# The inverse root mean square of eighteen norms, by one wide matmul and a power instead of column sums, Newton steps and a spread

## The chip, the cores and the metric

The kernel runs on one core of a Trainium2 chip. A core has a matmul engine (TensorE, in the profile PE, with its weight loads as PEld), VectorE (DVE), ScalarE (ACT), GpSimd (POOL) and SyncE (SP), which issues most of the DMAs. Each engine takes its instructions in order, and they wait for one another by semaphores. The metric is the device time of one execution in microseconds.

## The reference

One decoder layer in float32 with 2048 tokens (SEQ) and 1024 channels (D_MODEL). What matters here is that it has five RMS norms.

```python
def rmsnorm(x, g):
    xf = x.astype(jnp.float32)
    r = lax.rsqrt(jnp.mean(xf * xf, axis=-1, keepdims=True) + EPS)
    return (xf * r * g.astype(jnp.float32)).astype(x.dtype)

hn = rmsnorm(h, norm1_g)
proj = jnp.einsum('bsd,de->bse', hn, w_in)      # 512 pool channels, q, k, v
y_pool = pool_mixer(u_pool, pool_w, pool_scale)
o = stick_breaking_attention(to_heads(q), to_heads(k), to_heads(v))
mixed = jnp.concatenate([rmsnorm(y_pool, pool_out_g), rmsnorm(y_attn, attn_out_g)], axis=-1)
h = h + jnp.einsum('bse,ed->bsd', mixed, w_out)
hn2 = rmsnorm(h, norm2_g)
up = jnp.einsum('bsd,df->bsf', hn2, w_up)       # 4096 channels
act = jnp.square(jax.nn.relu(up))
h = h + jnp.einsum('bsf,fd->bsd', act, w_down)
return rmsnorm(h, final_g)
```

## The kernel before

The tokens are cut into four tiles of T = 512, and channels lie on the 128 partitions, so a tile of activations is a row of chunks of 128x512, one per 128 channels. Large products are made of float32r matmuls in three parts: `split` cuts an operand into a high and a low half (ScalarE rounds, line 143; VectorE subtracts, line 144), and a product is high x high, high x low and low x high.

The program runs in stages. The front (to about 500 us of the span) makes the input projection, the pool mixer and the attention of the four tiles, interleaved; the tail (to about 700 us) makes the output projection and the second norm; then `up` (to about 1290 us) and `down` (to the end) are the two halves of the feed-forward part, each a fast matrix multiplication of seven block products.

In front and tail the order is written by hand. `step` puts a dense product (`dense`, two granules of weights, 24 matmuls of 128x512 into one of two PSUM banks "pd") on a list; `run` goes through the list, and after each product `catch_up` takes a few pieces of elementwise work from the queue `later` (squares, norms, scaling of chunks), and `advance` a share of the attention. Weights are split five granules ahead (`WAHEAD`). A scheduler with a timeline of assumed costs then orders the instructions of each engine; `issue_after` and `gates` pin some of them: a gate makes the products that come a certain number of granules later wait for a norm's matmuls in the order of TensorE.

A norm goes so. The squares of the chunks are added up elementwise into `ss` (128x512), so that what is left is a sum over partitions, that is a column sum. `mean_squares` takes it with four float32 matmuls, each with 128 columns of `ss` as stationary side and a column of 1/n as moving side (line 199): the result `pm` is 128x4, tokens on partitions. `inv_root` adds the epsilon on VectorE (line 207) and takes the inverse root by a guess from the bits (line 208) and three Newton steps (lines 211 to 218), on the engine it is given. The result is cut into two float32r parts `yr` (lines 235 and 236), and `spread` (line 225) brings it back to all partitions with eight matmuls against the identity, in which the four columns are broadcast as stationary side; `pr` is 128x512, and ScalarE copies it to `r` in SBUF (line 245). VectorE then scales the chunks by gain and `r` (lines 257, 823, 917 and 1151).

There are 21 such roots: thirteen by `inv_rms` on GpSimd (front and tail), one by `inv_rms` on VectorE (the very first, in `norm1_first`), two by `root_last` for the two last tiles (their parts lie in `yrlast` until `up` spreads them, lines 1021 to 1024), three by `final_root` and `final_put` in `down`, and two halves of the last tile in `finish`, on VectorE, without a spread.

GpSimd has otherwise small copies (lines 371, 376 and 654) and, in `down`, the residual adds of `add_residual` (line 1096).

Of the kernel before, what the change touches and what calls it, by code (L numbers as in the profile page):

```python
# [8 lines left out]
F32 = mybir.dt.float32  # L9
F32R = mybir.dt.float32r  # L10
BF16 = mybir.dt.bfloat16
I32 = mybir.dt.int32
AF = mybir.ActivationFunctionType
ALU = mybir.AluOpType

P = 128
S = 2048
D = 1024
T = 512
# [8 lines left out]
TB = T // P  # L28
# [4 lines left out]
EPS = 1e-6  # L33
# [13 lines left out]
def hymba_block(ctx: ExitStack, tc: tile.TileContext, xT, gains, w_in, pool_w, w_out, w_up, w_down, out):  # L47
    nc = tc.nc
# [3 lines left out]
    const = pool("const", 1)  # L52
# [38 lines left out]
    open_big(left_scope)  # L91


    zero = ntp.tile([P, T], F32, tag="nt", name="zero")
    nc.vector.memset(zero, 0.0)
    ident = const.tile([P, P], F32, name="ident")
# [23 lines left out]
    zeros = const.tile([1, 1], I32, name="zeros")  # L120
    rlast = const.tile([P, 2, T], F32, name="rlast")
    sslast = const.tile([P, T], F32, name="sslast")
    yrlast = const.tile([P, 2, 2, TB], F32R, name="yrlast")
    carry = const.tile([P, len(WINDOWS), PAD], F32, name="carry")
    nc.vector.memset(carry, 0.0)

# [20 lines left out]
    marks, gates = {}, []  # L147
# [46 lines left out]
    def mean_squares(parts, n, where=None, tag="px"):  # L194

        pm = (where or psx).tile([P, T], F32, tag=tag, name="pm")
        for c in range(TB):
            for i, ss in enumerate(parts):
                marks["pm"] = nc.tensor.matmul(pm[:, c:c + 1], ss[:, c * P:(c + 1) * P], inv[n],  # L199
                                               start=(i == 0), stop=(i == len(parts) - 1))  # L200
        return pm[:, 0:TB]

    def inv_root(pm, eng):

        v, w = vp.tile([P, 3 * TB], F32, tag="v", name="v"), pm.shape[-1]
        m, y, t = v[:, 0:w], v[:, TB:TB + w], v[:, 2 * TB:2 * TB + w]
        nc.vector.tensor_scalar(m, pm, 1.0, EPS, op0=ALU.mult, op1=ALU.add)
        eng.tensor_scalar(y.bitcast(I32), m.bitcast(I32), -0.5, float(0x5F3759DF), op0=ALU.mult, op1=ALU.add)
        for _ in range(3):
            if eng is nc.vector:  # L210
                eng.scalar_tensor_tensor(t, y, -0.5, y, op0=ALU.mult, op1=ALU.mult)
                eng.tensor_tensor(t, t, m, ALU.mult)
                eng.scalar_tensor_tensor(y, t, 1.5, y, op0=ALU.add, op1=ALU.mult)
            else:
                eng.tensor_tensor(t, y, y, ALU.mult)
                eng.tensor_tensor(t, t, m, ALU.mult)
                eng.tensor_scalar(t, t, -0.5, 1.5, op0=ALU.mult, op1=ALU.add)
                eng.tensor_tensor(y, y, t, ALU.mult)
        return y

    def spread(pr, yr):

        for b in range(TB):
            for x in range(2):
                mm = nc.tensor.matmul(pr[:, b * P:(b + 1) * P], yr[:, x, b:b + 1].to_broadcast([P, P]), identr,  # L225
                                      start=(b == 0 and x == 0), stop=(b == TB - 1 and x == 1), skip_group_check=True)
        return mm

    def inv_rms(ss, n, r=None, eng=None, early=False):

        eng = eng or nc.gpsimd
        with tc.high_priority():
            y = inv_root(mean_squares([ss], n, psz if early else None, "pz" if early else "px"), eng)
            yr = tmp.tile([P, 2, TB], F32R, tag="yr", name="yr")
            eng.tensor_copy(yr[:, 0], y)
            eng.tensor_tensor(yr[:, 1], y, yr[:, 0].bitcast(F32), ALU.subtract)
            where, tag = (psx, "px") if eng is nc.vector else (psz, "pz") if early else (pst, "pt")
            pr = where.tile([P, T], F32, tag=tag, name="pr")
            marks["pr"] = spread(pr, yr)
            if eng is not nc.vector:  # L240
                g = state["tick"]
                gates.extend([(g + 10, marks["pm"]), (g + 14, marks["pr"])])
            if r is None:
                r = tmp.tile([P, T], F32, tag="r", name="r", bufs=2)
            nc.scalar.activation(r, pr, AF.Copy)
            return r

# [43 lines left out]
    todo, begun, finished, state = [], {}, set(), {"gran": 0, "tick": 0, "due": 0.0}  # L291
# [519 lines left out]
        return took  # L811

    def root_last(i, ss, where=None, tag="px"):
        y = inv_root(mean_squares([ss], D, where, tag), nc.gpsimd)
        nc.gpsimd.tensor_copy(yrlast[:, i, 0], y)
        nc.gpsimd.tensor_tensor(yrlast[:, i, 1], y, yrlast[:, i, 0].bitcast(F32), ALU.subtract)

    def norm2(j):
        acc = [st[j]["acc"][:, k] for k in range(KD)]
# [35 lines left out]
    def up(pools, more):  # L855
# [18 lines left out]
        def load(q, m):  # L874
            raw[q, m] = (rbb if m % 2 else rba).tile([P, 4, G, P], F32, tag="rb", name="rb")
            nc.sync.dma_start(raw[q, m], w_up[m])
# [9 lines left out]
        def make_weights(g):  # L886
            q, m, s = slots[g]
            which, i = what[s][1]
            if s == "P2":
                add_weights(q, m)  # L890
            hl = hlp.tile([P, 2, G, P], F32R, tag="hw", name="hw", align_bytes=256)
            split((hl[:, 0], hl[:, 1]), (sums if which else raw)[q, m][:, i])
            ops[g] = hl

        def make_left(q, s):
            i, parts = what[s][0], []
            for c in range(2):
                r = srp.tile([P, 2, T], F32, tag="sr", name="sr")
                nc.sync.dma_start(r, su[q][i][c])
                t = saps[order.index(s)].tile([P, 2, 2, T], F32R, tag="sa", name="sa", align_bytes=256)  # L900
                split((t[:, 0], t[:, 1]), r)
                parts.append(t)
            left_ops[q, s] = parts
# [97 lines left out]
        rbb, pup, avp, psu = more()  # L1001
        load(0, 1)
        lefts = [(g, q, s) for g, (q, m, s) in enumerate(slots) if m == 0 and not (q == 0 and s in order[:LB])]
        for g, (q, m, s) in enumerate(slots):
            while lefts and lefts[0][0] <= g + LA:
                make_left(*lefts.pop(0)[1:])
            if q == 0 and 4 <= m < 12 and m % 2 == 0 and s in SUMS:
                sums_second(m // 2 - 2, SUMS.index(s))
            bank, first, last = what[s][2:]
            if first:  # L1010
                ps[q, m, bank] = psu.tile([P, T], F32, tag=bank, name="p" + bank)
            t, w = ps[q, m, bank], ops.pop(g)
            for c in range(G):
                a = left_ops[q, s][c // 2]
                for x, (wx, ax) in enumerate(((0, 0), (0, 1), (1, 0))):
                    nc.tensor.matmul(t, w[:, wx, c], a[:, ax, c % 2], start=first and c == 0 and x == 0,  # L1016
                                     stop=last and c == G - 1 and x == 2, skip_group_check=True)
            post(q, m, s)
            if g == 1:
                root_last(1, sslast, psu, "R")  # L1020
            elif g in (6, 10):
                pr, i = psu.tile([P, T], F32, tag="R", name="pr"), g // 10
                spread(pr, yrlast[:, i])
                nc.scalar.activation(rlast[:, i], pr, AF.Copy)
            if g + UA < len(slots):
                make_weights(g + UA)
                q2, m2, s2 = slots[g + UA]
                n = q2 * NM + m2 + 2
                if s2 == "P3" and n < 2 * NM:
                    load(*cols[n])  # L1030

    def down(pools):
        t8, s8, rs, rt, pup, rsp, rlp, tmp_, psb = pools
# [103 lines left out]

        def final_root(j, acc, ss, r):

            y = inv_root(mean_squares([ss], D, psb, f"b{free}"), nc.gpsimd)  # L1140
            yr = tmp_.tile([P, 2, TB], F32R, tag="yr", name="yr", bufs=3)
            nc.gpsimd.tensor_copy(yr[:, 0], y)
            nc.gpsimd.tensor_tensor(yr[:, 1], y, yr[:, 0].bitcast(F32), ALU.subtract)
            roots.append((j, acc, r, yr))

        def final_put(j, acc, r, yr):
            pr = psb.tile([P, T], F32, tag=f"b{free + 1}", name="pr")
            spread(pr, yr)
            nc.scalar.activation(r, pr, AF.Copy)
            for k in range(KD):  # L1150
                nc.vector.scalar_tensor_tensor(acc[k], acc[k], gf[:, k:k + 1], r, op0=ALU.mult, op1=ALU.mult)
                nc.sync.dma_start(out[j, k], acc[k])

        finals, roots, lastv = [], [], {}
# [80 lines left out]
        free, held = 4, []  # L1235
        for g in range(DA):
            make(g)
        for g, (n_, i, kk, qs_) in enumerate(steps):
            if g + DA < len(steps):
                make(g + DA)  # L1240
            t, left_ = made.pop(g)
# [3 lines left out]
            for q in qs_:  # L1245
                for n in range(4):
                    if kk == 0 and n_ in ("P1", "P5", "P2"):
                        ps[q, n] = bank(4 * q + n)
                    for c in range(2):
                        for x, (wx, ax) in enumerate(((0, 0), (0, 1), (1, 0))):  # L1250
                            nc.tensor.matmul(ps[q, n], t[:, wx, c, n * P:(n + 1) * P], left_[q][:, ax, c],  # L1251
                                             start=(n_ in ("P1", "P5", "P2") and kk == 0 and c == 0 and x == 0),
                                             stop=(n_ in ("P4", "P3", "P2") and kk == 7 and c == 1 and x == 2),
# [3 lines left out]
            if n_ == "P2":  # L1257
                if qs_ == (1,):
                    free = 0
# [169 lines left out]
```

## Time and profile before

| | |
|---|---|
| median of 3 runs | 1945.07 us (1943.7 to 1950.17) |
| span of the profiled execution | 1941.4 us; the page gives no separate time for it |
| PE busy | 1922.7 us, 99% |
| DVE busy | 1267.6 us, 65% |
| ACT busy | 956.9 us, 49% |
| POOL busy | 192.0 us, 10% |
| DMA | 426.79 MB, mean 220 GB/s |
| granted TensorE clock | 0.998 of full speed |

The profile is of one execution. A row of a tile or a line has the count, the durations in ns and the first and last start in us; a row of the chain has the start, the length and the work that carried the end in that time; a row of the timeline has start, length, engine, line, operation, output and inputs, and in brackets the idle time of the engine before it.

### The profile page before, as it was taken

The numbers are of one execution on the slowest core, as the hardware profiler recorded it, in microseconds if no ns is written. First come the engines' busy times: TensorE is split into PE (matmuls) and PEld (weight loads), VectorE is DVE, ScalarE is ACT, GpSimd is POOL, SyncE is SP. The second block draws the span as 40 slices with busy tenths as digits, with TensorE's granted clock in tenths as the row PEclk, the third lists the DMA queues.
The fourth block names the chain that finished last, engine by engine and source line by source line (L and its number), as shares of the span: only waits on it lengthen the run. The fifth ranks groups of instructions, "written<-read, shape, count | busy, mean of one in ns | idle before, by whom it ended". The sixth has DMA issues, their size and how long they took to land.

```text
span 1941.4 us, 25998 instructions
## 1 busy us (share of the span) xinstructions
PE 1922.7 (99%) x9139; PEld 1605.2 (83%) x9139; DVE 1267.6 (65%) x1882; ACT 956.9 (49%) x1544; POOL 192.0 (10%) x399
## 2 busy tenths in 40 slices
PE   9999999999999999999999999999999999999997
PEld 7888888888888888888888888878888888888887
DVE  6887799668876975777586565665454443446474
ACT  5565566455544555555575555553323233424353
POOL 0211123102111110000000000000110000213010
PEclk9999999999999999999999999999999999999999
DMA  6685686888696954677564544477885554546472
GB/s 216 206 273 180 223 279 208 266 307 285 235 378 233 338 187 155 213 243 247 181 243 159 173 141 158 145 268 288 290 284 196 192 196 151 201 153 208 148 255 89
DMA packets 164845, 426.79 MB, mean 220 GB/s; under 512 B 19680, under 2 KB 25824, under 8 KB 160608
## 3 DMA queue, kind: packets, MB, share of 16 engines
q1 hardware_dynamic: 164560, 424.77, 64.1%
q8 instruction: 74, 1.21, 0.3%
q14 instruction: 67, 0.55, 0.1%
q10 hardware_dynamic: 144, 0.26, 0.0%
HBM read 284.44 MB, written 140.51 MB: 219 GB/s over the span
## 4 chain that ended last, share of the span: by engine, by line
PE 94%; DVE 3%; DMA 2%; ACT 1%; issue 0%; SPq 0%; DVEq 0%; ACTq 0%
PE pb L1251 31%; PE pY L1016 17%; PE pd L173 8%; PE pd L172 8%; PE pd L174 8%; PE pZ L1016 8%; PE pX L1016 4%; PE po L669 2%; PE pta L658 1%; PE pm L199 1%; PE pz L611 1%; PE pz L612 1%; PE pr L225 1%; DMA wr<-in_w_down_dram 1%; PE pb L1214 1%; PE pz L640 0%
## 5 line engine op out<-in xcount | busy, mean ns | idle before, releaser
L1251 PE MATMUL pb<-ad,wd 128*128 128x512 f32 x2640 | 601.6, 390 | 1.3 <-ACT ad L143 0.7
L1251 PEld LDWEIGHTS pb<-ad,wd 128*128 128x128 f32 x2640 | 494.8, 188 | 104.6 <-ACT ad L143 1.3
L1016 PE MATMUL pY<-sa,hw 128*128 128x512 f32 x1536 | 364.3, 390 | 1.2 <-ACT u L955 1.2
L1016 PEld LDWEIGHTS pY<-sa,hw 128*128 128x128 f32 x1536 | 288.1, 188 | 61.8 <-ACT u L955 2.1
L172 PE MATMUL pd<-h,hl 128*128 128x512 f32 x752 | 299.8, 399 | 0.7 <-DVE qkr L418 0.7
L173 PE MATMUL pd<-h,hl 128*128 128x512 f32 x752 | 297.2, 395 | 0.0
L174 PE MATMUL pd<-h,hl 128*128 128x512 f32 x752 | 297.0, 395 | 0.0
L143 ACT ACTIVATE ad<-ar 128x1024 fp32r<-128x1024 f32 x112 | 117.4, 1051 | 139.4 <-PE pb L1251 116.7
L1016 PE MATMUL pZ<-sa,hw 128*128 128x512 f32 x768 | 184.6, 389 | 0.0
L144 DVE TENSOR_TENSOR ad<-ar,ad 128x1024 fp32r<-128x1024 f32 x112 | 144.3, 1293 | 55.6 <-ACT ad L143 55.6
L144 DVE TENSOR_TENSOR wd<-wr,wd 128x1024 fp32r<-128x1024 f32 x64 | 82.2, 1285 | 148.9 <-ACT wd L143 148.4
L143 ACT ACTIVATE wd<-wr 128x1024 fp32r<-128x1024 f32 x64 | 67.8, 1059 | 206.0 <-PE pb L1251 198.3
L1016 PEld LDWEIGHTS pZ<-sa,hw 128*128 128x128 f32 x768 | 144.1, 188 | 29.8
L172 PEld LDWEIGHTS pd<-h,hl 128*128 128x128 f32 x752 | 142.2, 189 | 28.3 <-DVE qkr L418 1.0
L174 PEld LDWEIGHTS pd<-h,hl 128*128 128x128 f32 x752 | 141.9, 189 | 27.9
L173 PEld LDWEIGHTS pd<-h,hl 128*128 128x128 f32 x752 | 142.0, 189 | 26.8
L143 ACT ACTIVATE hl<-raw 128x512 fp32r<-128x512 f32 x168 | 104.2, 630 | 108.2 <-PE pd L174 69.9
L144 DVE TENSOR_TENSOR hl<-raw,hl 128x512 fp32r<-128x512 f32 x168 | 114.6, 687 | 51.3 <-ACT hl L143 50.9
L144 DVE TENSOR_TENSOR hw<-rt,hw 128x512 fp32r<-128x512 f32 x128 | 87.7, 688 | 76.3 <-ACT hw L143 76.1
L1016 PE MATMUL pX<-sa,hw 128*128 128x512 f32 x384 | 93.1, 389 | 0.0
L1046 DVE TENSOR_TENSOR wr<-wr 128x1024 f32<-128x1024 f32 x32 | 39.2, 1224 | 81.0 <-DMA wr<-in_w_down_dram 78.0
L955 ACT ACTIVATE u<-pY 128x512 f32<-128x512 f32 x64 | 38.1, 595 | 103.6 <-PE pY L1016 103.3
(203 smaller groups left out, 2389.7 us busy)
## 6 DMA issues: line engine op xcount, KB each, us to landing
ar<-sd SPq DMA_DIRECT2D x112, 512.0 KB, 4.5
wr<-in_w_down_dram SPq DMA_DIRECT2D x72, 512.0 KB, 3.7
rb<-in_w_up_dram SPq DMA_DIRECT2D x32, 1024.0 KB, 6.1
sd<-a SPq DMA_DIRECT2D x128, 256.0 KB, 3.7
raw<-in_w_in_dram SPq DMA_DIRECT2D x50, 512.0 KB, 4.4
sd<-s SPq DMA_DIRECT2D x96, 256.0 KB, 3.8
raw<-in_w_out_dram SPq DMA_DIRECT2D x32, 512.0 KB, 5.6
sr<-su SPq DMA_DIRECT2D x28, 512.0 KB, 5.5
```

The costliest lines, as they stand in the source:

```text
L143: nc.scalar.activation(hi, src, AF.Copy)
L144: return nc.vector.tensor_tensor(lo, src, hi.bitcast(F32), ALU.subtract)
L172: nc.tensor.matmul(ps, hl[:, 0, c], hi, start=(k == 0), stop=False)
L173: nc.tensor.matmul(ps, hl[:, 0, c], lo, start=False, stop=False)
L174: mm = nc.tensor.matmul(ps, hl[:, 1, c], hi, start=False, stop=(k == n - 1))
L199: marks["pm"] = nc.tensor.matmul(pm[:, c:c + 1], ss[:, c * P:(c + 1) * P], inv[n], start=(i == 0), stop=(i == len(parts) - 1))
L225: mm = nc.tensor.matmul(pr[:, b * P:(b + 1) * P], yr[:, x, b:b + 1].to_broadcast([P, P]), identr, start=(b == 0 and x == 0), stop=(b == TB ...
L669: nc.tensor.matmul(po[:, p * 256 + to:p * 256 + to + hi - lo], vw[:, 2 * p + v], at[:, x, lo:hi], start=(p == 0 and n == 0 and x == 0), sk ...
L955: nc.scalar.activation(k[name], y, AF.Copy)
L1016: nc.tensor.matmul(t, w[:, wx, c], a[:, ax, c % 2], start=first and c == 0 and x == 0, stop=last and c == G - 1 and x == 2, skip_group_che ...
L1046: nc.vector.tensor_tensor(b, a, b, ALU.subtract)
L1251: nc.tensor.matmul(ps[q, n], t[:, wx, c, n * P:(n + 1) * P], left_[q][:, ax, c], start=(n_ in ("P1", "P5", "P2") and kk == 0 and c == 0 an ...
```

## The change

For the eighteen roots that ran on GpSimd, `mean_root` replaces `mean_squares`, `inv_root`, the parts `yr` and `spread`. A constant 128x128 matrix with 1/n everywhere is the stationary side of one float32 matmul with `ss` as moving side, so that every partition of `pm` (128x512) has the mean square of each token. ScalarE copies it to `r` and adds the epsilon, and GpSimd raises `r` to the power of -0.5 in place, with a constant column broadcast as exponent. The bank for `pr` and its gate fall away, and the roots of the last two tiles are complete at once in `rlast`. The first norm and the halves of the last tile stay as they were.

```diff
+    mean = {}
+    for n in (D, D // 2):
+        mean[n] = const.tile([P, P], F32, name=f"mean{n}")
+        nc.gpsimd.memset(mean[n], 1.0 / n)
+    root = const.tile([P, 1], F32, name="root")
+    nc.gpsimd.memset(root, -0.5)
...
-    yrlast = const.tile([P, 2, 2, TB], F32R, name="yrlast")
...
+    def mean_root(ss, n, r, where, tag):
+
+        pm = where.tile([P, T], F32, tag=tag, name="pm")
+        marks["pm"] = nc.tensor.matmul(pm, mean[n], ss, start=True, stop=True)
+        nc.scalar.activation(r, pm, AF.Copy, bias=EPS)
+        nc.gpsimd.tensor_tensor(r, r, root.to_broadcast([P, T]), ALU.pow)
+
     def inv_rms(ss, n, r=None, eng=None, early=False):
 
-        eng = eng or nc.gpsimd
         with tc.high_priority():
+            if eng is None:
+                if r is None:
+                    r = tmp.tile([P, T], F32, tag="r", name="r", bufs=2)
+                mean_root(ss, n, r, psz if early else psx, "pz" if early else "px")
+                gates.append((state["tick"] + 10, marks["pm"]))
+                return r
             y = inv_root(mean_squares([ss], n, psz if early else None, "pz" if early else "px"), eng)
...
-            where, tag = (psx, "px") if eng is nc.vector else (psz, "pz") if early else (pst, "pt")
-            pr = where.tile([P, T], F32, tag=tag, name="pr")
-            marks["pr"] = spread(pr, yr)
-            if eng is not nc.vector:
-                g = state["tick"]
-                gates.extend([(g + 10, marks["pm"]), (g + 14, marks["pr"])])
...
     def root_last(i, ss, where=None, tag="px"):
-        y = inv_root(mean_squares([ss], D, where, tag), nc.gpsimd)
-        nc.gpsimd.tensor_copy(yrlast[:, i, 0], y)
-        nc.gpsimd.tensor_tensor(yrlast[:, i, 1], y, yrlast[:, i, 0].bitcast(F32), ALU.subtract)
+        mean_root(ss, D, rlast[:, i], where or psx, tag)
...
             if g == 1:
                 root_last(1, sslast, psu, "R")
-            elif g in (6, 10):
-                pr, i = psu.tile([P, T], F32, tag="R", name="pr"), g // 10
-                spread(pr, yrlast[:, i])
-                nc.scalar.activation(rlast[:, i], pr, AF.Copy)
...
         def final_root(j, acc, ss, r):
 
-            y = inv_root(mean_squares([ss], D, psb, f"b{free}"), nc.gpsimd)
...
+            mean_root(ss, D, r, psb, f"b{free}")
+            roots.append((j, acc, r))
+
+        def final_put(j, acc, r):
...
```

More of the change, by code (lines that the diff above doesn't have):

```diff
@@ L209, in inv_root @@
         for _ in range(3):
[L210 to L218, printed above, removed]
+            eng.scalar_tensor_tensor(t, y, -0.5, y, op0=ALU.mult, op1=ALU.mult)
+            eng.tensor_tensor(t, t, m, ALU.mult)
+            eng.scalar_tensor_tensor(y, t, 1.5, y, op0=ALU.add, op1=ALU.mult)
         return y
@@ L236, in inv_rms @@
             eng.tensor_tensor(yr[:, 1], y, yr[:, 0].bitcast(F32), ALU.subtract)
-            where, tag = (psx, "px") if eng is nc.vector else (psz, "pz") if early else (pst, "pt")
-            pr = where.tile([P, T], F32, tag=tag, name="pr")
-            marks["pr"] = spread(pr, yr)
-            if eng is not nc.vector:
-                g = state["tick"]
-                gates.extend([(g + 10, marks["pm"]), (g + 14, marks["pr"])])
-            if r is None:
-                r = tmp.tile([P, T], F32, tag="r", name="r", bufs=2)
+            pr = psx.tile([P, T], F32, tag="px", name="pr")
+            spread(pr, yr)
             nc.scalar.activation(r, pr, AF.Copy)
@@ L1138, in final_root @@
         def final_root(j, acc, ss, r):
-            y = inv_root(mean_squares([ss], D, psb, f"b{free}"), nc.gpsimd)
[L1141 to L1149, printed above, removed]
+            mean_root(ss, D, r, psb, f"b{free}")
+            roots.append((j, acc, r))
+        def final_put(j, acc, r):
             for k in range(KD):
```

## The prediction

> **What bounds the kernel now.** I read the page's busy table and its chain first, to see which engine sets the end.
>
> ```profile
> span 1941.4 us, 25998 instructions
> PE 1922.7 (99%) x9139; PEld 1605.2 (83%) x9139; DVE 1267.6 (65%) x1882; ACT 956.9 (49%) x1544; POOL 192.0 (10%) x399
> PE 94%; DVE 3%; DMA 2%; ACT 1%; issue 0%; SPq 0%; DVEq 0%; ACTq 0%
> ```
>
> TensorE (PE) is busy for 99% of the span and carries 94% of the chain that ended last. A microsecond taken out of TensorE's stream is a microsecond off the end, as long as nobody else becomes late. So the first question is what the norms cost on TensorE, and the second is who could become late. For the second I cut the span by stage and keep the stretch that holds most of the norms, 30 to 660 us. The columns after the length are busy time of PE, weight loads, DVE, ACT and POOL, then granted clock, DMA share and GB/s.
>
> ```profile
> 30.00:660.00 630.00, 626.35 (x3342) 532.62 (x3343) 504.18 (x852) 346.18 (x625) 110.58 (x281) 1.00 0.77 256
> ```
>
> There VectorE (DVE) is busy 504.18 of 630 us, 80%: it has 126 us of idle time in this stretch, and it is the only engine near PE.
>
> **How many norms the change touches.** The rows of the tiles pm and v count them. In the rows of a tile the three numbers are minimum, median and maximum in ns.
>
> ```profile
> L199 PE MATMUL pm<-inv,ss x144: 165/250/251, 29.5 to 1895.9; 128*128 128x1 f32 x144
> L199 PE MATMUL pm<-inv,sslast x8: 164/250/251, 702.2 to 702.9; 128*128 128x1 f32 x8
> L207 DVE TENSOR_SCALAR v<-pm x19: 136/157/164, 31.0 to 1896.2; 128x4 f32<-128x4 f32 x19
> L208 POOL TENSOR_SCALAR v<-v x18: 192/193/2301, 63.3 to 1896.5; 128x4 int32<-128x4 int32 x18
> L218 POOL TENSOR_TENSOR v<-v x54: 198/199/1507, 64.4 to 1901.6; 128x4 f32<-128x4 f32 x54
> ```
>
> Nineteen norms read pm with VectorE; eighteen of them run their Newton steps on GpSimd (POOL): thirteen through inv_rms, two through root_last, three through final_root. Those eighteen change. The first norm and the two halves of the last tile keep Newton on VectorE. A second thing stands here: 19 norms times 4 column sums are 76 matmuls in the code, and 152 in the trace. A float32 matmul is two TensorE instructions, where the float32r ones are one.
>
> **What is removed on TensorE.** The chain gives what these groups displace, which is less than the durations, because matmuls overlap. Columns: start, length, what.
>
> ```profile
> 177.43 0.79 PE pm L199 x8
> 694.66 2.72 PE pY L1016 x12
> 1895.32 0.79 PE pm L199 x8
> 1904.38 0.06 PE pr L225
> 1904.72 0.73 PE pr L225 x7
> ```
>
> Eight column-sum instructions take 0.79 us, and eight spread matmuls take 0.06 + 0.73 = 0.79 us. Both sit on the chain, in the middle of the work. Each of the eighteen norms so gives back 1.58 us, 28.4 us together.
>
> **What is added on TensorE.** One float32 matmul of 512 columns per norm. No float32 matmul of that width is in the trace, so I bound it. A float32r matmul of 512 columns takes 2.72 / 12 = 0.227 us of the stream. Two instructions at that rate are 0.45 us: the lower end. The upper end is my estimate from the doubled count: if float32 is worked as two parts, and the two instructions are the two parts of the stationary side, the moving side may have to pass twice as well, four passes of 0.227 us, 0.91 us. The one-column matmuls cannot show it, their columns being too few. I take the upper end, since the doubled instructions show that the array does split this type. The sum is 18 x (1.58 - 0.91) = 12.1 us saved; by the lower end, 18 x (1.58 - 0.45) = 20.3 us.
>
> The Trainium skill says in "FP8 and Floating Point Precision", section TensorE Precision Notes, that true float32 takes four passes through the array; by it the sum is the same 12.1 us, and no row here shows more than the two instructions.
>
> **The other engines' small change.** Durations for this part, from the rows of r, and the timeline of GpSimd and ScalarE after the last of these norms (first and last of its fifteen GpSimd instructions):
>
> ```profile
> L245 ACT ACTIVATE r<-pr x12: 583/598/601, 39.1 to 625.1; 128x512 f32<-128x512 f32 x12
> 1896.47 0.19 POOL L208 TENSOR_SCALAR v<-v 128x4 int32<-128x4 int32 x1 [34.02 <-DVE v L207]
> 1902.12 0.20 POOL L1143 TENSOR_TENSOR yr<-v,yr 128x4 fp32r<-128x4 f32 x1
> 1905.49 0.60 ACT L1149 ACTIVATE rf<-pr 128x512 f32<-128x512 f32 x1 [1.82 <-PE pr L225]
> ```
>
> ScalarE (ACT) copied pr to r in 0.6 us; now it copies pm to r with the epsilon in 0.6 us: nothing. VectorE loses 18 x 0.157 = 2.8 us of L207, hidden under PE. GpSimd loses fifteen small instructions per norm, 5.9 us from first to last here. TensorE loses a wait on GpSimd in its in-order queue; it cost nothing, since the spread was queued late enough. Before, r was ready 10.8 us after the column sums began (1895.32 to 1906.09). The two memsets of the mean matrices run on GpSimd at the very start, where nothing but later transposes needs what follows them: nothing.
>
> **The power.** One GpSimd instruction, 128x512, two inputs, per norm. No power is in the trace. The nearest row is the residual add, of the same engine, shape and number of inputs:
>
> ```profile
> L1096 POOL TENSOR_TENSOR u<-u,res x16: 1279/1322/2209, 1673.4 to 1773.3; 128x512 f32<-128x512 f32 x16
> L1096 POOL TENSOR_TENSOR c<-c,res x8: 1288/1296/2293, 1650.4 to 1668.8; 128x512 f32<-128x512 f32 x8
> ```
>
> It cannot be shorter than the add's 1.28 us, which reads and writes the same amounts. For the upper end I take as many passes of the add as the Newton chain has arithmetic steps (one guess, three rounds of four, the epsilon): 14 x 1.28 = 18 us; a power needs a logarithm and an exponential, which are series of about such a length. These ends are far apart. I take 5 us, their geometric mean, because neither end has a row of this operation.
>
> With 5 us the new latency is 0.9 + 0.6 + 5 = 6.5 us, less than 10.8, so no consumer of r is later than before. What else it can hurt is VectorE. These rows show the residual adds beside VectorE's splits, whose normal time is the median in the first:
>
> ```profile
> L144 DVE TENSOR_TENSOR ad<-ar,ad x112: 1207/1219/2312, 1310.8 to 1899.4; 128x1024 fp32r<-128x1024 f32 x112
> 1661.39 2.22 DVE L144 TENSOR_TENSOR wd<-wr,wd 128x1024 fp32r<-128x1024 f32 x1 [0.74 <-ACT wd L143]
> 1663.53 4.55 DVE L144 TENSOR_TENSOR ad<-ar,ad 128x1024 fp32r<-128x1024 f32 x2
> 1661.22 3.54 POOL L1096 TENSOR_TENSOR c<-c,res 128x512 f32<-128x512 f32 x2 [1.97 <-DMA res<-hs]
> 1665.20 1.79 POOL L1096 TENSOR_TENSOR c<-c,res 128x512 f32<-128x512 f32 x1 [0.44 <-DMA res<-hs]
> ```
>
> While GpSimd adds, a split that takes 1.22 us takes 2.2 to 2.3, and the add in turn 1.8 instead of 1.3. Each waits out the other. So I price the power as time in which VectorE's two-input work stands still. Behind it in VectorE's in-order queue wait the evacuations of TensorE's result banks and the splits of the weights. The front has two banks for its dense products, and one bank's product is 24 matmuls, 24 x 0.227 = 5.4 us: a standstill below that is covered. Five us is covered, just. In total thirteen such standstills are 65 us, half of the 126 us that VectorE has idle there.
>
> The Trainium skill speaks against the change here: "SBUF — State Buffer", section Who interferes with whom, says that a VectorE instruction with two SBUF inputs and a GpSimd instruction that reads SBUF exclude each other for the whole instruction. The stretched splits agree, 2.2 to 2.3 us against 1.22; whether a GpSimd instruction many times longer than an add also holds VectorE all that time, no row here shows.
>
> **Sum.** 28.4 us removed, 16.3 us added, 12.1 us saved. The page gives the profiled execution's span, 1941.4 us, and no separate time; the median of the runs is 1945.07, 3.7 us longer. Against the span the forecast is 1929.3, against the median 1933.0 us. About 0.3% (5.8 us) is what a measurement of this kernel tells from no change. If only the power's and the matmul's favourable ends hold, it is 1925; if some of the covers slip, up to 1939: that is the likeliest case's own range.
>
> **Rivals.**
>
> *The power stops VectorE (slower).* If the power lasts longer than the 5.4 us cover, each of the thirteen norms of the front holds PE for the rest. Break-even is where 13 x (X - 5.4) eats 12.1 us: X = 6.3 us. At 10 us the price is 13 x 4.6 = 60 us, net +48: 1993 us. At 18 us it is 13 x 12.6 = 164, net +152: 2097 us, and the five later norms, whose weights are split further ahead, would add to it. For it: VectorE's 80% and the stretched splits, and my upper end for X. Against it: a standstill needs the power to hold its port throughout, and GpSimd instructions of 128x4 cost VectorE nothing visible.
>
> *The saving is eaten in the front (no change).* TensorE's saving counts only where PE is the bound. If VectorE at 80% sets the pace around the thirteen front norms, because the standstill just cancels the gain, five norms remain: 5 x 0.67 = 3.4 us, 1942 us. For it: the power's time near the break-even; against it: PE is busy 626 of 630 us there.
>
> *The wide matmul takes only two passes (faster by more).* 20.3 us: 1925 us. For it: two instructions; against it: the split itself. It lies in the forecast's own range.
>
> *Another order of the instructions.* The order is planned from assumed costs; a power planned too short puts its consumer, VectorE's scaling of the chunks, directly behind it, and VectorE waits in order. If each of the eighteen waits cost 1 us more than now beyond the saving, the time would be 1933 + 18 = 1951 us.
>
> **How the numbers follow.** The forecast with its two-pass variant gets 0.48. The cancelling case gets 0.12. Slower through VectorE's standstill 0.34, of which about half lies beyond 10 us of power; the unlucky order 0.06. So faster 0.48, same 0.12, slower 0.40. The predicted time is the likeliest case's, 1933. The range begins at 1924, just below the two-pass case, and reaches 2000, a power of a little over 10 us; what lies beyond is about 0.17.
>
> **What would show it.** Right: pm as 18 pairs of 128x512 float32 matmuls, each norm at 0.91 us in the chain; no L225 but the first norm's; PE's busy time down by about 12 us at an unchanged 99%; power instructions on GpSimd of about 5 us; splits of VectorE stretched by up to that, PE without new waits. Wrong: power instructions above 6.3 us with VectorE's two-input instructions stretched to their length, PE below 99% between 30 and 660 us, and waits of PE on VectorE's splits or evacuations. A matmul pair at 0.45 us would show the two-pass case; VectorE waiting for GpSimd's r without stretched splits, the unlucky order.

## The result and the profile after

The changed kernel takes 2940.22 us (median of 5 runs, 2936.26 to 2943.51) against 1945.07 us before: a ratio of 1.5114, 95% interval 1.5093 to 1.5135. It is 995 us slower where 12 us faster was forecast.

From the page of the changed kernel: span, busy times, and the groups of the power (busy time in us, mean in ns, and idle time of the engine before, with what ended it).

```profile
span 2938.4 us, 25216 instructions
PE 1959.5 (67%) x8887; PEld 1608.7 (55%) x8887; DVE 1284.0 (44%) x1864; ACT 961.6 (33%) x1544; POOL 1573.7 (54%) x150
L233 POOL TENSOR_TENSOR r<-r,root 128x512 f32<-128x512 f32 x11 | 902.8, 82069 | 26.6 <-ACT r L232 25.3
L233 POOL TENSOR_TENSOR rf<-rf,root 128x512 f32<-128x512 f32 x3 | 246.6, 82232 | 66.3 <-ACT rf L232 66.3
L233 POOL TENSOR_TENSOR ra<-ra,root 128x512 f32<-128x512 f32 x2 | 164.1, 82029 | 20.5 <-DMA acc<-in_xT_dram 20.5
L233 POOL TENSOR_TENSOR rlast<-rlast,root 128x512 f32<-128x512 f32 x2 | 163.8, 81924 | 0.0
```

One power of 128x512 takes 82 us. Eighteen of them are 1477 us of GpSimd, which had 192 us of work before. TensorE has as many large matmuls as before, but is busy for 67% of the span, not 99%; VectorE and ScalarE have hardly more work than before. So engines wait. These are the rows of the tiles pY and pb, before (first three) and after, whose first and last starts mark the stages: the first pY begins the feed-forward part, the first pb its second half, the last pb ends TensorE's large work.

```profile
L1016 PE MATMUL pY<-sa,hw x1536: 387/389/500, 694.5 to 1305.4; 128*128 128x512 f32 x192
L1251 PE MATMUL pb<-ad,wd x2640: 387/389/501, 1309.2 to 1915.7; 128*128 128x512 f32 x189
L1214 PE MATMUL pb<-ad,wd x96: 278/283/368, 1916.0 to 1929.4; 128*128 128x256 f32 x96
L1019 PE MATMUL pY<-sa,hw x1536: 387/389/793, 1506.0 to 2145.1; 128*128 128x512 f32 x192
L1244 PE MATMUL pb<-ad,wd x2640: 389/389/798, 2149.4 to 2752.1; 128*128 128x512 f32 x189
L1207 PE MATMUL pb<-ad,wd x96: 277/283/284, 2752.3 to 2763.7; 128*128 128x256 f32 x96
```

| stage | before, us | after, us | difference |
|---|---|---|---|
| front and tail, to the first pY | 694.5 | 1506.0 | +811.5 |
| `up`, to the first pb | 614.7 | 643.4 | +28.7 |
| `down`, to the last pb | 620.2 | 614.3 | -5.9 |
| the end, to the end of the span | 12.0 | 174.7 | +162.7 |

Front and tail hold thirteen powers and lose 811 us, 62 for each. Six powers, the last four of the thirteen and the two of `root_last`, run without a gap from 1151.7 to 1643.3 us: there GpSimd's own 82 us for each root set the pace. `up` loses 29 us, 23.6 of them in one wait of TensorE that ends just behind the second `root_last` power. The end loses 163 us: three powers run one after the other, and the last two of them run when TensorE has nothing left to do. In `down` alone, where the first of them is hidden, the change gains.

What a power does in the front is seen best in one. Timeline of the changed kernel around the third power; columns start, length, engine, line, operation, output and inputs, idle time before it and its releaser.

```profile
304.68 81.92 POOL L233 TENSOR_TENSOR r<-r,root 128x512 f32<-128x512 f32 x1 [1.21 <-DVE pl L389]
307.02 0.68 DVE L149 TENSOR_TENSOR pls<-pl,pls 128x512 fp32r<-128x512 f32 x1
...
331.57 0.69 DVE L149 TENSOR_TENSOR hl<-raw,hl 128x512 fp32r<-128x512 f32 x1 [2.02 <-ACT hl L148]
386.55 0.20 POOL L376 COPY u<-carry 128x15 f32<-128x15 f32 x1
386.68 0.20 POOL L381 COPY carry<-u 128x15 f32<-128x15 f32 x1
386.63 2.11 DVE L262 SCALAR_TENSOR_TENSOR nt<-xt,gains,r 128x512 f32<-128x512 f32 x3 [54.37 <-POOL r L233]
386.91 0.60 ACT L380 ACTIVATE u<-pd 128x512 f32<-128x512 f32 x1 [55.38 <-POOL carry L381]
387.56 0.79 PE L177 MATMUL pd<-h,hl 128*128 128x512 f32 x1 [56.69 <-ACT u L380]
```

For 27 us of the power the engines go on, and VectorE's splits, with two inputs in SBUF, take 0.68 us as ever. Then two queues stop, at about the same time. VectorE has come to the first scaling of a chunk (nt), which reads r, and stands for 54 us; all its later work is behind it. ScalarE has come to an evacuation into a tile u, whose last reader is the small copy into carry (L381), and that copy stands on GpSimd behind the power; ScalarE stands for 55 us. TensorE has no free bank for its next product and stands for 57 us. After that its matmuls of 128x512 take 0.63 to 0.79 us until 393 us, instead of 0.39. The granted clock of the whole span, 0.998 before, is 0.828 after: 0.73 up to the first pY and 1.00 in `down`.

### The profile page after: what moved, and what is told of

Read it like the earlier page. It is cut to its first block, busy times and chain, and to the rows that moved or that the text cites. A ratio compares the mean times of both kernels' runs of the same rounds, so it can differ in the third digit from the quotient of the medians.

```text
span 2938.4 us, 25216 instructions
## 1 busy us (share of the span) xinstructions
PE 1959.5 (67%) x8887; PEld 1608.7 (55%) x8887; DVE 1284.0 (44%) x1864; ACT 961.6 (33%) x1544; POOL 1573.7 (54%) x150
## 5 line engine op out<-in xcount | busy, mean ns | idle before, releaser
L233 POOL TENSOR_TENSOR r<-r,root 128x512 f32<-128x512 f32 x11 | 902.8, 82069 | 26.6 <-ACT r L232 25.3
L177 PE MATMUL pd<-h,hl 128*128 128x512 f32 x752 | 313.0, 417 | 499.2 <-ACT h L148 224.4
L177 PEld LDWEIGHTS pd<-h,hl 128*128 128x128 f32 x752 | 149.3, 199 | 535.5 <-ACT h L148 225.7
L1095 POOL TENSOR_TENSOR p<-p,res 128x512 f32<-128x512 f32 x8 | 11.7, 1468 | 602.6 <-ACT p L1101 586.2
L178 PE MATMUL pd<-h,hl 128*128 128x512 f32 x752 | 308.1, 410 | 2.4 <-DVE h L149 2.3
L179 PE MATMUL pd<-h,hl 128*128 128x512 f32 x752 | 305.9, 407 | 0.0
L233 POOL TENSOR_TENSOR rf<-rf,root 128x512 f32<-128x512 f32 x3 | 246.6, 82232 | 66.3 <-ACT rf L232 66.3
L1019 PE MATMUL pZ<-sa,hw 128*128 128x512 f32 x768 | 187.3, 392 | 23.7 <-DVE a L972 23.6
L233 POOL TENSOR_TENSOR ra<-ra,root 128x512 f32<-128x512 f32 x2 | 164.1, 82029 | 20.5 <-DMA acc<-in_xT_dram 20.5
L178 PEld LDWEIGHTS pd<-h,hl 128*128 128x128 f32 x752 | 148.6, 198 | 37.2 <-DVE h L149 6.0
L179 PEld LDWEIGHTS pd<-h,hl 128*128 128x128 f32 x752 | 147.9, 197 | 32.4 <-issue 1.4
L233 POOL TENSOR_TENSOR rlast<-rlast,root 128x512 f32<-128x512 f32 x2 | 163.8, 81924 | 0.0
```

The source lines that it names most:

```text
L177: nc.tensor.matmul(ps, hl[:, 0, c], hi, start=(k == 0), stop=False)
L178: nc.tensor.matmul(ps, hl[:, 0, c], lo, start=False, stop=False)
L179: mm = nc.tensor.matmul(ps, hl[:, 1, c], hi, start=False, stop=(k == n - 1))
L233: nc.gpsimd.tensor_tensor(r, r, root.to_broadcast([P, T]), ALU.pow)
L1095: nc.gpsimd.tensor_tensor(t, t, r, ALU.add)
```

## The experiments

Three theories of the loss stood against each other. *Wait*: VectorE's reader of r stands in its in-order queue. *Lock*: VectorE's two-input work stands still while a power runs, as the prediction had it. *Queue*: small copies stand behind the power on GpSimd. A fourth, that the wide matmul or the new order costs time by itself, had to be cleared first.

**The change without the power's time (e1_short).** The epsilon goes, and the norms are not computed.

```diff
-        nc.scalar.activation(r, pm, AF.Copy, bias=EPS)
-        nc.gpsimd.tensor_tensor(r, r, root.to_broadcast([P, T]), ALU.pow)
+        nc.scalar.activation(r, pm, AF.Sigmoid, scale=5.0)
+        nc.gpsimd.tensor_tensor(r, r, one.to_broadcast([P, T]), ALU.mult)
...
```

> The changed kernel with the power replaced by a multiplication by one on GpSimd, of the same shape; so that the values stay finite and near one, ScalarE takes the sigmoid of five times the mean square from pm instead of copying it (no epsilon): the norms are left out, all instructions' places stay. Three theories of the 995 us: (wait) VectorE's first reader of r waits in its in-order queue for the long power; (lock) VectorE's work with two SBUF inputs stands still during the power; (queue) the small copies behind the power in GpSimd's queue come late. All three put the whole loss on the power's 82 us and expect about 1933 us here, 12 us below before, with each wide matmul at 0.91 us of TensorE's stream (1925 us if it is 0.45). A rival, that the wide matmul or the new order of instructions costs time by itself, expects 1950 us or more.

Measured: 1931.30 us against 1945.70 of before on the same chip, ratio 0.9922 (0.9905 to 0.9938): 14.4 us faster. From its chain, one wide matmul in the middle of the front, start, length, what; and from its tile r, the multiplication (minimum, median, maximum in ns):

```profile
177.46 0.86 PE pm L233 x2
L235 POOL TENSOR_TENSOR r<-r,one x11: 1035/1040/1369, 61.1 to 604.6; 128x512 f32<-128x512 f32 x11
```

Two instructions displace 0.86 us. By the prediction's own sum 18 x (1.58 - 0.86) = 13.0 us. So the whole loss hangs on the length of the power, and the rest of the change is worth 14 us.

**A power that nobody reads (e2_unread, e2_inplace).** Both leave the norms out as e1_short does.

```diff
+            nc.gpsimd.tensor_tensor(where_unread, one.to_broadcast([P, T]), root.to_broadcast([P, T]), ALU.pow)
...
```

> As e1_short, with the full 82 us power added on GpSimd behind the multiplication in sixteen of the eighteen norms (not in the two that wait for the feed-forward part), on constant data and into a tile that nobody reads. Theory wait expects the time of e1_short, within some 10 us. Theory lock expects VectorE's two-input instructions of up to 80 us, and about the changed kernel's 2940 us less what root_last cost, some 2800 us. Theory queue expects normal VectorE instructions, but waits of VectorE and ScalarE for the copies into u, carry and left that stand behind the power: 13 norms of the front times some 20 to 60 us, 2200 to 2700 us.

Measured: 2652.12 us (one run). The experiment did not do what it was built for: with nothing to wait for, the powers were planned one behind the other from 1.6 us on, with only small GpSimd work between, so they do not stand where those of the change stand. The second one takes r as input.

```diff
+            nc.gpsimd.tensor_tensor(unread, r, root.to_broadcast([P, T]), ALU.pow)
...
```

> e2_unread had its unread powers moved together to the start by the planner, since they waited for nothing. Here the unread power takes r after the multiplication as its input, in the thirteen norms of front and tail, so that it begins where the changed kernel's did; its output is still read by nobody. Theory wait alone (VectorE's first reader of r stands in its queue): within 15 us of e1_short's 1931. Theory queue alone (copies behind the power on GpSimd): most of the thirteen times 82 - 26 us of the changed kernel's loss, 2400 to 2700 us. Both at work: between these, some 2100 to 2400 us.

Measured: 2493.43 us (one run), 562 above e1_short. VectorE's waits (for what, us in total, times, longest), and the splits of the weights:

```profile
DVE s L390 <- POOL u L380: 151.5, 3, 61.4
DVE pc L632 <- POOL left L663: 112.8, 6, 40.3
L151 DVE TENSOR_TENSOR hl<-raw,hl x168: 656/692/694, 5.3 to 1076.8; 128x512 fp32r<-128x512 f32 x168
```

The longest of these splits is 0.694 us, with thirteen powers beside them: a power does not hold VectorE for its length. It does so at its beginning, as the run e6_copies below shows best:

```profile
59.25 82.03 POOL L233 TENSOR_TENSOR r<-r,root 128x512 f32<-128x512 f32 x1 [56.92 <-ACT r L232]
59.41 1.53 DVE L149 TENSOR_TENSOR hl<-raw,hl 128x512 fp32r<-128x512 f32 x1
```

The split that starts 0.16 us behind the power takes 1.53 us instead of 0.69. In the changed kernel 13 of VectorE's 21 instructions that start within the first 1.2 us of a power are stretched, to 1.53 us at most, and none of the 516 that start later beside it. So the theory lock holds for the first one or two of the 82 us, and not for the rest.

VectorE waits in e2_inplace for the copies into u and left, which stand behind the powers; seven pauses of TensorE lead back to these copies, 302 us together. So the queue alone costs hundreds of us. Its first pY starts at 1147.8 us against 683.3 in e1_short: 464 us lost up to there. That is not the copies alone: from 949 us on the powers stand one behind the other, and the multiplications of later norms wait behind them too. The other 98 us come later, where ScalarE waits 52.0 us for a power before a split (sa), and 44.6 us before it writes rlast, into which the unread powers write. That part belongs to the experiment.

**The small copies on VectorE (e6_copies).** Everything is computed.

```diff
-        nc.gpsimd.tensor_copy(u[:, 0:PAD], carry[:, g])
+        nc.vector.tensor_copy(u[:, 0:PAD], carry[:, g])
...
-            nc.gpsimd.tensor_copy(left[j][:, 2 * p:2 * p + 2, h], pc2[:, :, 0])
+            nc.vector.tensor_copy(left[j][:, 2 * p:2 * p + 2, h], pc2[:, :, 0])
```

> The changed kernel, powers of 82 us and read as they are, with the three small copies (into u, carry and left) on VectorE instead of GpSimd, so that in the front nothing but powers is in GpSimd's queue. It computes everything. Theory queue alone: the loss of the front goes, about 2100 to 2200 us is left (the two roots before the feed-forward part and the three at the end). Theory wait alone: 2940 us as before, less nothing, since VectorE still waits in order for r. Both: the longer of two overlapping waits stays, 2700 to 2950 us.

Measured: 2837.96 us (one run), 102 below the changed kernel. Its waits of VectorE for roots:

```profile
DVE nt L262 <- POOL r L233: 378.6, 9, 72.9
DVE nt L262 <- POOL ra L233: 111.6, 2, 75.7
DVE p L1144 <- POOL rf L233: 75.7, 1, 75.7
```

Its first pY starts at 1401.1 us. So up to there the loss is 1401 - 683 = 718 us with the copies out of GpSimd's queue, 464 with the queue alone, and 823 with both (1506 - 683). The copies stand on VectorE here, behind its own waits, so the 718 us are not quite the wait alone. The two overlap: in the timeline above VectorE and ScalarE stop within a microsecond of each other, and freeing one leaves the other. The waits of the changed kernel itself tell which is the larger:

```profile
DVE nt L262 <- POOL r L233: 477.9, 9, 71.9
ACT u L380 <- POOL carry L381: 140.8, 3, 55.4
PE pd L177 <- ACT u L380: 144.2, 3, 56.7
```

Up to the first pY TensorE stands still in twelve long pauses, 747 us together. VectorE waits for a root in each of them. ScalarE waits for a copy in three, 144 us of TensorE's time, and e6_copies, which frees the copies, gains 105 us up to there.

**How long may the power be (e3_w32, e3_w64, e3_w128).** After the multiplication of e1_short, a power of only the first w columns; the norms stay left out.

```diff
+        nc.gpsimd.tensor_tensor(r[:, 0:32], r[:, 0:32], root.to_broadcast([P, 32]), ALU.pow)
...
```

> As e1_short, with a power of the first 32 columns of r behind the multiplication: at 160 ns for a column (81.92 us / 512) 5.1 us, and 6.5 us with the multiplication, just above the break-even of 6.3 us that the prediction worked out from VectorE's standstill. Theory lock: 13 x (6.5 - 5.4) = 14 us lost of the 12 gained, about 1947 us. Theory wait: r comes about 8 us after the matmul begins, earlier than the 10.8 us of before, so nothing is lost: within 4 us of e1_short.

> As e3_w32 with the power on 64 columns: 1.0 + 64 x 0.16 + 0.3 = 11.6 us on GpSimd per norm, r ready 13 us after the matmul begins, 2 us later than before. Theory lock: 13 x (11.6 - 5.4) = 81 us lost, about 2012 us. Theories wait and queue: within what the banks and split weights cover, 1931 to 1945 us.

> As e3_w32 with the power on 128 columns: 21.8 us on GpSimd per norm. The changed kernel lost (2940 - 1931) / 18 = 56 us for each power of 82, that is, as if 26 us of each were covered. If the cover is a fixed 26 us: about 1935 us here. If it is the 5.4 us of the two result banks beyond the latency of before: r is 12.6 us later than before, 13 x 7.2 = 94 us, about 2025 us.

```profile
L236 POOL TENSOR_TENSOR r<-r,root x11: 5413/5415/5801, 61.8 to 607.2; 128x32 f32<-128x32 f32 x11
L236 POOL TENSOR_TENSOR r<-r,root x11: 10522/10788/10979, 62.2 to 638.7; 128x64 f32<-128x64 f32 x11
L236 POOL TENSOR_TENSOR r<-r,root x11: 20710/20717/21167, 61.3 to 720.9; 128x128 f32<-128x128 f32 x11
```

These are one row of the tile r of each. With the full width of 81.92 us the length is a straight line, (81.92 - 5.41) / 480 = 0.159 us for a column and 0.3 us to begin; 64 columns, at 10.5 to 11.0 us, lie on it or a little above.

| | on GpSimd per norm, us | time, us | above e1_short, us |
|---|---|---|---|
| e1_short | 1.0 | 1931.30 | 0 |
| e3_w32 | 6.5 | 1936.98 | 5.7 |
| e3_w64 | 11.8 | 1956.94 | 25.6 |
| e3_w128 | 21.8 | 2042.23 (one run) | 111 |
| the change | 82 | 2940.22 | 1009 |

Against before the ratios are 0.9964 (0.9951 to 0.9976) for 32 columns and 1.0056 (1.0036 to 1.0076) for 64; the break-even lies between 6.5 and 11.8 us. The theory lock missed where it was priced (1947 and 2012 us). Of my other numbers, that of 32 columns was too low by 2 us and that of 64 by 12, and at 128 the fixed cover of 26 us is refuted, the 2025 us of the two banks is nearer. There is no fixed cover: a microsecond more costs 1.0 us below 6.5, 3.8 us up to 11.8, 8.5 us up to 21.8 and 14.9 us beyond, which is most of the eighteen norms. That fits a slack of its own for each norm, used up one after the other; the slack of single norms was not measured.

**The power on four columns (e4_narrow).** The kernel before, column sums and spread kept, and one power of 128x4 in place of Newton. Everything is computed.

```diff
+        if eng is nc.gpsimd:
+            eng.tensor_tensor(y, m, root.to_broadcast([P, w]), ALU.pow)
+            return y
...
```

> The kernel before, with its column sums and spread, and one power on the 128x4 means in place of the guess and the three Newton steps on GpSimd: at 160 ns for a column and 0.3 us to begin about 0.9 us instead of thirteen instructions over some 5 us. It computes everything. TensorE's work is that of before, so if TensorE's stream is the bound: the same as before within 4 us. If the latency of the root matters by itself: faster by up to 10 us.

Measured: 1947.77 us against 1946.82, ratio 1.0014 (1.0003 to 1.0025), within the 0.3% that count as no change.

```profile
L211 POOL TENSOR_TENSOR v<-v,root x18: 1007/1009/3125, 61.9 to 1900.4; 128x4 f32<-128x4 f32 x18
```

GpSimd's thirteen instructions have become one of 1.0 us, and the end does not move: GpSimd's chain was hidden, and taking it away gains nothing by itself.

**The wide matmul with other roots (e5_sqrt, e7_lnexp, e8_arsqrt).** All three compute the norms in full.

```diff
-        nc.scalar.activation(r, pm, AF.Copy, bias=EPS)
-        nc.gpsimd.tensor_tensor(r, r, root.to_broadcast([P, T]), ALU.pow)
+        nc.scalar.activation(r, pm, AF.Sqrt, bias=eps)            # e5_sqrt
+        nc.vector.reciprocal(r, r)
+        nc.scalar.activation(r, pm, AF.Ln, bias=eps)              # e7_lnexp
+        nc.scalar.activation(r, r, AF.Exp, scale=-0.5)
+        nc.scalar.activation(r, pm, AF.Abs_reciprocal_sqrt, bias=eps)   # e8_arsqrt
...
```

> The changed kernel with no power: ScalarE takes the square root of pm plus epsilon into r, and VectorE its reciprocal in place. It computes the norm in full. If only the power was wrong with the change, about 1933 to 1938 us: 12 us of TensorE saved, 18 x 0.6 us more on VectorE, hidden, and table loads on ScalarE if the square root needs another table than the sigmoid of the attention, some 1 to 3 us per norm, hidden unless they delay an evacuation. If the wide matmul costs more than I think: 1945 us or more.

> The changed kernel with the root on ScalarE alone: the logarithm of pm plus epsilon, and the exponential of -0.5 times it, two instructions of 128x512 in place of the copy and the power. It computes the norm in full. e5_sqrt gave back its 14 us through VectorE's reciprocal, 3.35 us each; if that was the reason, this one keeps them: 1931 to 1936 us, with 18 x 0.7 us more on ScalarE and one to three table loads of 1.3 us a norm. If the table loads late in ScalarE's queue cost as much as the reciprocals: 1940 us or more.

> As e7_lnexp with one ScalarE instruction, the inverse root of the absolute value of pm plus epsilon, and so no second pass: 1929 to 1934 us if its table loads are hidden. It computes the norm in full, as exactly as that function's table does.

Measured: e5_sqrt 1945.65 us against 1945.70, ratio 0.9993 (0.9983 to 1.0003); e7_lnexp 1937.87 against 1946.82, 0.9959 (0.9948 to 0.9970); e8_arsqrt 1929.33 against 1946.82, 0.9921 (0.9904 to 0.9937). From the tile r of e5_sqrt, and ScalarE's table loads at the lines of the root in e7_lnexp (two lines) and in e8_arsqrt (one line, the same in e5_sqrt), busy time and mean ns:

```profile
L235 DVE RECIPROCAL r<-r x11: 3344/3352/3353, 63.3 to 619.3; 128x512 f32<-128x512 f32 x11
L234 ACT ACT_TABLE_LOAD x18 | 23.1, 1283 | 0.7 <-PE pm L233 0.4
L235 ACT ACT_TABLE_LOAD x18 | 23.1, 1283 | 0.3
L234 ACT ACT_TABLE_LOAD x9 | 11.5, 1283 | 0.6 <-PE pm L233 0.4
```

In e5_sqrt the reciprocal, which I had priced at 0.6 us, takes 3.35 us of VectorE, and the 14 us are gone: with VectorE at 80% in the front, 18 x 3.35 = 60 us were not all hidden. The table loads are not the reason, since e8_arsqrt has as many and no reciprocal, and keeps its gain; nor is the wide matmul, which the expectation would have blamed, by the 0.86 us of e1_short. In e7_lnexp the expectation was missed by 2 us; it has two table loads of 1.28 us in each norm. e8_arsqrt has half as many instructions, nine loads at its line instead of 36, and it is the fastest kernel here that computes the norms: 17.5 us below before. Why that is more than the 13.0 us of TensorE's sum is not shown.

## Why the prediction was wrong

*TensorE as the bound, and its sum: right.* 12.1 us were forecast, from 0.91 us for the wide matmul; the matmul takes 0.86, and the rest of the change without the power's time is worth 14.4 us. The estimate of four passes, worked from the doubled instructions, was the right end of its bounds. The Trainium skill's four passes ("FP8 and Floating Point Precision", TensorE Precision Notes) agree with the 0.86 us, which is 3.8 of 0.227.

*The power: this step failed.* It was bounded by 1.28 and 18 us and taken at 5. It takes 81.9 us, sixteen times the value taken, 4.5 times the upper end and 64 times the add. The lower end was the row of an add. The upper end was no row at all, but the assumption that a power is as many full passes of an add as the Newton chain has steps; no run shows of what steps it is made. It is 160 ns for a column, where the add of 1.28 us takes 2.5. The text said that neither end has a row of this operation, and then took a mean of the two, as if the middle of an unknown were likely; and the range stopped at a power of a little over 10 us although 18 was still inside the bounds.

*What a long power holds up: wrong mechanism.* The main rival had VectorE's two-input work stand still. Behind the first microseconds of a power it does not: the splits take 0.68 to 0.69 us beside it. The stretched splits beside the residual adds, 2.2 us instead of 1.22, were read rightly, but do not carry over to this instruction. On this the Trainium skill ("SBUF — State Buffer", Who interferes with whom) says that the two exclude each other for the whole instruction; the trace does not agree for the power, which stretches only what starts in its first 1.2 us. The rival's price, 13 x (X - 5.4), is 996 us at 82 us. That this is the whole measured loss, 995, is luck: it is a price of front and tail, which lost 811, and at 21.8 us it is 213 where 111 was measured. By the prediction's own list of signs, VectorE waiting for r without stretched splits meant the unlucky order.

*The wait for r: right in kind, wrong in size.* It was the rival of the unlucky order, VectorE in order behind its own reader of r, at 1 us a norm; in e6_copies, with the copies out of GpSimd's queue, 718 us are lost up to the first pY, 55 for each of the thirteen. The work behind the power on GpSimd, mostly small copies and 464 us by itself, was not in the prediction at all, though the rows of lines 371, 376 and 654 stood among the instructions of that queue: a step put on an engine's queue had to be priced against what else stands in that queue.

*The end: not priced.* Of the five later norms the prediction said only that their weights are split further ahead and that they would add to the loss. The last two have no cover at all: their powers run after TensorE's last product, and the end is 163 us longer.

*ScalarE's copy at nothing, Newton's removal at nothing: right as far as shown.* e4_narrow shows the second by itself; the first is borne out only by e1_short, which has a ScalarE instruction of the same shape there and gains the whole sum.

## What to carry to other kernels

An operation that has no row in the trace can be far from its nearest row, here 64 times it; a change that hangs on one deserves a measurement of that instruction alone before its place is argued about, and until then a range that reaches to where it would decide. A long instruction on an idle engine is not free: it holds its own reader, everything behind that reader in an in-order queue, and everything behind itself. When a step that takes work off the bound engine loses, it can pay to keep that part and look for another home for the rest: the wide matmul with the inverse root on ScalarE is 17.5 us faster than before.

## What the runs showed of the hardware that was not expected

A power on GpSimd takes 0.159 us for a column of 128 float32 plus about 0.3 us: 1.0 us for 4 columns, 5.4 for 32, 81.9 for 512; and it holds up VectorE's instructions only at its beginning: those that start in its first 1.2 us take up to 1.53 us instead of 0.7, while later splits of 128x512 take their normal 0.68 to 0.69. Beside them the power itself takes 81.9 to 82.7 us (changed kernel). A reciprocal of 128x512 on VectorE takes 3.35 us. A float32 matmul of 512 columns takes 0.86 us of TensorE's stream, 3.8 times a float32r one.
